# Sums of weight blocks issued behind the convolution's first closed token tile, or in the first feed-forward projection

## The chip, the cores and the metric

The kernel runs on one core of one Trainium2 chip. The metric is the device time of one execution in microseconds (us); the time of the kernel is the median over its runs. Engine names are those of the profile: PE multiplies matrices, PEld loads its weights, DVE, ACT and POOL compute, SP issues most of the loads from memory. POOL also issues transfers, in the same queue as its few computing instructions.

## The reference

Two layers over a residual stream of 512 tokens x 1024 features, all in float32. Layer 0 mixes with a gated short convolution, layer 1 with sliding-window attention; behind each mixer stands a gated feed-forward block.

```python
mix = short_conv_mixer(rmsnorm(h, a_pre_norm[l]), a_w_in[l], a_conv_w[l], a_w_out[l])
h = h + rmsnorm(mix, a_post_norm[l])
...
ff = swiglu(rmsnorm(h, ffn_pre_norm[l]), ffn_w_gate_up[l], ffn_w_down[l])
h = h + rmsnorm(ff, ffn_post_norm[l])
```

The change lies between the last product of layer 0's convolution (`y @ a_w_out`) and the first product of layer 0's feed-forward block (`rmsnorm(h) @ ffn_w_gate_up`).

## The kernel before

**Arithmetic.** Each float32 operand is split into a high and a low part (`whi`, `wlo`, `xhi`, `xlo`), and three products are added (`mm3`, L208 to L210). Most large products are made as seven block products instead of eight, which needs sums and differences of weight blocks. These sums are made in device memory by transfers alone: `Sums` holds, for one group of weights, two or four sum tiles (`hsum`), and a list of steps. The first step copies weight blocks into the sum tiles, the second adds other blocks to them (a transfer that accumulates), and two more steps add sums to sums where four are kept. A step must find the one before it landed.

**What sets when the sums are made.** `sum_on(at)` is called at named places. It issues what is left in `issues`, begins the sum group that the table `BEGIN` names for that place, and appends the next step of every open group to `issues`; these are issued by a later `issue` or `sum_on`. All of them go out on POOL's queue, on line L570, and are kept in program order. At `"o0"`, ahead of the convolution's closing, the group `g04` begins (gate weights, two sum tiles): its two copies are issued. At `"o1"` come the two accumulating transfers of `g04`, and the four copies of `d01` (a group of the down projection, four sum tiles): six transfers. At `"0f0"` comes the second step of `d01`, two accumulating transfers, which go out at the next place.

**The closing.** `close` multiplies the rest of the convolution's output with its weights, token tile by token tile (four tiles of 128 tokens, two halves of 512 features each; PE tile `pmix`). Each half is added to `mix` (`take`, L278, DVE) and squared on ACT (L283). `tile_done(t)` then runs, in this order:

```python
if t > 0: res.mean2(t - 1)   # uv L335 on DVE, then ur L339 on POOL
res.scale(t, 0)              # mix L309 on DVE
res.mean(t)                  # uv L312 on DVE, then ur L317 on POOL
if t > 0: res.norm(t - 1)    # xn L344 on ACT
res.scale(t, 1)
res.update(t)                # h L322 on DVE; kept L327 on SP's queue
if square: res.square(t)     # junk L330 on ACT
```

(comments by this text; `mean2` and `mean` take the power -1/2 of a mean square on POOL.) `mean` gives the factor with which tile t enters the residual stream, `mean2` the factor by which the updated tile is normalised into `xn`. So each of the four tiles sends two instructions of one column to POOL. In the last tile's second half PE does half of its products, then transposes `xn` of tiles 0 and 1 (`turn`, L355, 16 transposes into the banks `xt`), then the other half. ACT and DVE split the transposed tiles into high and low parts (`split`, L368 and L369).

**The first feed-forward projection.** `last_tile` finishes tiles 2 and 3 on the other engines while `project_first` runs plain products (PE tile `pgu`) over the first 256 tokens (`hf == 0`), block of features by block of features (`k`), and then over the last 256 (`hf == 1`); its callback `then(hf, k)` puts transposes and splits between. After that `in_line` runs a line of jobs, each with weight tiles (`raw`, fetched on SP's queue, L466) that are split on ACT (L499) and DVE (L500) three jobs ahead.

**Order.** On PE, DVE, ACT and POOL the instructions around the change stand in the order in which the code writes them. SP's queue is set by a scheduler.

Of the kernel before, what the change touches and what calls it, by code (L numbers as in the profile page):

```python
# [83 lines left out]
def yoco_kernel(  # L84
# [39 lines left out]
    def name(s):  # L124
        uid[0] += 1
        return f"{s}_{uid[0]}"
# [13 lines left out]
    def bank(s, pool=None):  # L140

        if pool is None:
            pool = (ps_mm, ps_sc, ps_mm, ps_pt)[turn[0] % 4]
            turn[0] += 1
        return pool.tile([P, S], F32, tag="bank", name=name(s))
# [413 lines left out]
    issues = []  # L559

    def issue(n, behind=None):

        for dst, src, op in issues[:n]:
            if len(dst.shape) == 3:
                dst, src = (t.rearrange("k (a b) c -> (k a) (b c)", b=4) for t in (dst, src))
            else:
                dst, src = (t.rearrange("(a b) c -> a (b c)", b=2) for t in (dst, src))
            kw = {} if op is None else {"accum_op": op}
            made = tc.keep_in_program_order(
                nc.gpsimd.dma_start(dst, src, max_dma_last_dim=4 * 4 * S, **kw))  # L570
            if behind is not None:
                tc.add_manual_dep(
                    made.ins, behind.ins.name, mybir.DependencyInfo(
                        mybir.DependencyClass.Sync, mybir.DependencyReason.DATA),
                    reason="pace")
        del issues[:n]
# [13 lines left out]
    def sum_on(at, behind=None):  # L590

        issue(len(issues), behind)
        if at in BEGIN:
            summing.append(sums_of[BEGIN[at]])
        for x in summing:
            x.step()
        summing[:] = [x for x in summing if x.steps]
# [38 lines left out]
    def seven(acts, n, mix, first):  # L636
# [9 lines left out]
        def product(p, ks, hi, lo):  # L646
# [35 lines left out]
    ws = [[wsp.tile([P, D], F32R, tag=tag, name=name(tag)) for tag in ("whi", "wlo")]  # L682
          for _ in range(3)]
# [104 lines left out]
    ws = [split_weights(None, raw, True) for raw in later[:2]]  # L788
# [33 lines left out]
    ys, acts, mix_c = [], [], [None] * NB  # L822
    both = []
    res = Update(mix_c, B_CONV, [G_FPRE[0]])
# [231 lines left out]
    ws = [line[f"w{n}"].w for n in range(4)]  # L1056
# [13 lines left out]
        if square:  # L1070
            res.square(t)

    def close(ws, x, k0, res, ahead, then=None, each=2, sooner=False):


        n = len(x) - k0

        def part(ps, t, half, ks):
            unit(ps, t, ws[len(ws) // 2 * half :], x, ks, n, k0)

        begun = [bank("pmix", ps_mm) for _ in range(2)]
        for half in range(2):
            part(begun[half], 0, half, range(n - 1))
            for _ in range(each if half == 0 or each > 1 else 0):
                ahead.one()
        for t in range(NB):
            for half in range(2):
                if t == 0:
                    ps = begun[half]
                    part(ps, t, half, range(n - 1, n))  # L1090
                else:
                    ps = bank("pmix", ps_mm)
                    if (t, half) == (NB - 1, 1):
                        lead = 3 if sooner else 2
                        part(ps, t, half, range(lead))
                        for ts in ((0,), (1,)) if sooner else ((0, 1),):
                            for b in range(4):
                                res.turn(b, ts)
                        part(ps, t, half, range(lead, n))
                        if sooner:  # L1100
                            res.split(0, 0, 0)
                            res.take(t, 0, last)
                            res.split(0, 1, 0)
                            res.take(t, 1, ps)
                            res.split(0, 2, 0)
                            res.split(0, 3, 0)
                            res.square_mix(t, 0)
                            res.square_mix(t, 1)
                            res.square(NB - 2)
                            continue  # L1110
                        for f in range(4):
                            res.split(0, f, 0)
                        res.square_mix(t, 0)
                        res.square(NB - 2)
                        res.scale(t, 0)
                    else:
                        part(ps, t, half, range(n))
                        if sooner and t == NB - 1:
                            last = ps
                            continue  # L1120
                res.take(t, half, ps)
                if (t, half) != (NB - 1, 0):
                    res.square_mix(t, half)
            if t < NB - 1:
                tile_done(res, t, square=t < NB - 2)
            if t == 0 and then:
                then()

    def last_tile(res, pieces, ahead=None):

# [42 lines left out]
    issue(len(issues))  # L1173
    ahead = Ahead(first_weights(0))
    with tc.manual_schedule(engines=ALL):

        def sums_on():
            sum_on("o1")
            issue(len(issues))

        close(ws, ys, 0, res, ahead, sums_on)


    def ffn(l, before, ahead, gain, gpres, following):
# [5 lines left out]
        def gate_pair(pg, pu):  # L1190
# [12 lines left out]
            return pair_sums(gr, acts[0])  # L1203

        def gate_jobs(q, factors, out, to, then):


# [141 lines left out]
        with tc.manual_schedule(engines=ALL):  # L1349
            last_tile(before, [  # L1350
                [(0, 4)], [(0, 5), ("keep", 0, False), ("weights",)],
                [], [("keep", 1, True), (0, 6), (0, 7), ("keep", 3, True)],
                [("keep", 2, False), ("weights",)]], ahead)

            def then(hf, k):
                if hf == 0 and k in (5, 6):
                    for b in ((0, 1), (2, 3))[k - 5]:
                        before.turn(b, (2,))
                if hf == 0 and k == 6:
                    for b in range(4):  # L1360
                        before.turn(b, (3,))
                    for f in range(KT):
                        before.split(0, f, 1)
                    for b in range(4):
                        before.keep(b, 1)
                if hf == 1 and k == 1:
                    factors.update(before.factors())
                if hf == 1 and k == 3:
                    sum_on(f"{l}f0")

            factors = {}
            project_first(pss, ahead.ready[:4], xs, then)

            def late():
                parts = [gate_pair(*pss[i : i + 2]) for i in (0, 2)][1]
                sum_on(f"{l}f1")
                return parts

            jobs, behind_one = [], []
            for rd, (f0, f1) in enumerate(ROUNDS):  # L1380
                last = rd == len(ROUNDS) - 1
                for f in range(max(f0, PLAIN), f1, 2):
                    q = (f - PLAIN) // 2
                    jobs += gate_jobs(q, factors, pair_acts if last else pair_sums, acts[rd],
                                      lambda q=q: sum_on(f"{l}p{q}"))
                    if behind_one and not (last and f < f1 - 2):
                        jobs += behind_one.pop()
                if last:
                    break
                down = down_jobs(range(f0 // 2, f1 // 2), acts[rd], rd == 0,  # L1390
                                 sums_of[f"d{l}{rd}"],
                                 lambda rd=rd: sum_on(f"{l}s{rd}"))
                behind_one.append(down)
            n = f1 - f0

            def weights(half, j):
                return w_dn[l, half : 4 - half : 3 - 2 * half, f0 // 2 + j]


            closing = [Job([Raw(weights(half, j))], None) for half in range(2) for j in range(2)]  # L1400
            for at, job in zip(LAST, closing):
                job.slots = True
                jobs.insert(len(jobs) - at, job)
            in_line(jobs, late)
            if l == 1:
                nc.gpsimd.drain()
        res = Update(mix, gain, gpres)
# [5 lines left out]
        ws = [job.w for job in closing]  # L1413
        if gpres:
            ahead = Ahead(following)
# [32 lines left out]
    res, ahead = ffn(0, res, ahead, B_FFN[0], [G_KV, G_BPRE], [  # L1448
        w_k[0], w_k[1], w_v[:, 0:D], w_v[:, D:], w_q[0], w_q[1]])
# [327 lines left out]
    with tc.manual_schedule(engines=ALL):  # L1777
        sum_on("a0")
        for i in range(KT + 2):
            if i == KT:  # L1780
                res = Update(mix_o, B_ATT, [G_FPRE[1]])
                res.leaves = True
                ahead = Ahead(first_weights(1))
# [5 lines left out]
            for c in order.split():  # L1789
# [18 lines left out]
                t = i - late  # L1808
# [19 lines left out]
                else:  # L1828
                    t = 2 * (t - EARLY - 1) + n.pop(0)
# [110 lines left out]
```

## Time and profile before

| | us |
|---|---|
| median of 3 runs | 1013.61 (1011.48 to 1014.05) |
| profiled execution | 1012.63 |
| its span, first to last instruction | 1010.9 |
| PE busy in it | 1000.5 |
| DVE, ACT, POOL busy | 911.2, 609.0, 182.9 |
| granted PE clock, mean | 0.998 of full |
| closing of the convolution (`pmix`) on PE | from 153.2 to about 179 |

The profiled execution took 1.7 us more than its span and 1.0 us less than the median. Times of single instructions are counted from the span's start. A busy PE counts each product to its modelled end, so that overlapping products make it look full.

### The profile page before, as it was taken

The page shows a single profiled execution, that of the slowest core. Times are in us where ns is not written, and L with a number is a line of the kernel's source. Part 1 is how long each engine was busy: PE and PEld are TensorE (multiplying, and loading weights), DVE is VectorE, ACT ScalarE, POOL GpSimd, SP SyncE. Part 2 cuts the span into 40 slices and gives each one's busy share as a digit, 9 for nine tenths or more (in the row PEclk, how much of TensorE's full clock was granted, in tenths as well). Part 3 has the DMA queues.
Part 4 walks back from the last instruction along what each step waited for, and adds up shares of the span by engine and source line. Part 5 has one row for each costly group of instructions (what it writes and reads, how often), then busy time and mean ns, then how long its engine had stood idle before and what let it go on. Part 6 is the DMA issues. An engine that isn't in the chain of part 4 may idle for free.

```text
span 1010.9 us, 16458 instructions
## 1 busy us (share of the span) xinstructions
PE 1000.5 (99%) x6008; PEld 887.4 (88%) x6008; DVE 911.2 (90%) x1564; ACT 609.0 (60%) x1105; POOL 182.9 (18%) x250
## 2 busy tenths in 40 slices
PE   9999999999999999999999999999999999999997
PEld 8899887999889898898898888789998888989986
DVE  7798876899789999999888998988997999999996
ACT  8345544875656465566385788777666564645641
POOL 0211022102101011000022657321211010110001
PEclk9999999999999999999999999999999999999999
DMA  9886989649979789779603889966999576979742
GB/s 353 265 239 179 334 285 319 199 167 270 341 235 286 252 286 311 238 219 341 209 1 121 225 223 258 293 242 173 306 294 316 167 250 233 295 264 275 242 170 83
DMA packets 67728, 246.61 MB, mean 244 GB/s; under 512 B 8000, under 2 KB 8512, under 8 KB 55872
## 3 DMA queue, kind: packets, MB, share of 16 engines
q1 hardware_dynamic: 52480, 148.07, 39.3%
q0 software_dynamic: 14592, 96.48, 37.3%
q8 instruction: 47, 0.77, 0.3%
q10 hardware_dynamic: 576, 1.02, 0.3%
q14 instruction: 33, 0.27, 0.1%
HBM read 239.25 MB, written 102.76 MB: 338 GB/s over the span
## 4 chain that ended last, share of the span: by engine, by line
PE 93%; DMA 3%; DVE 2%; ACT 1%; POOL 1%; issue 0%; DVEq 0%; ACTq 0%
PE gx L1284 15%; PE gx L1287 8%; PE px L208 4%; PE px L209 4%; PE px L210 4%; DMA hsum<-in_w_gb_dram 3%; PE gz L1284 3%; PE pmix L210 2%; PE gy L209 2%; PE gy L208 2%; PE gy L210 2%; PE pmix L208 2%; PE pmix L209 2%; PE pz L209 2%; PE pz L208 2%; PE pz L210 2%
## 5 line engine op out<-in xcount | busy, mean ns | idle before, releaser
L500 DVE TENSOR_TENSOR wlo<-raw,whi 128x1024 fp32r<-128x1024 f32 (+1 forms) x231 | 279.3, 1214 | 27.6 <-ACT whi L499 27.4
L499 ACT ACTIVATE whi<-raw 128x1024 fp32r<-128x1024 f32 (+1 forms) x231 | 239.7, 1051 | 79.1 <-DVE raw L487 37.7
L1284 PE MATMUL gx<-xt,whi 128*128 128x512 f32 x480 | 120.6, 393 | 0.0
L1284 PEld LDWEIGHTS gx<-xt,whi 128*128 128x128 f32 x480 | 86.2, 189 | 15.7
L570 POOL DMA_DIRECT2D hsum<-in_w_gb_dram x96 | 63.7, 730 | 167.8 <-ACT whi L499 107.6
L570 POOL DMA_DIRECT2D hsum<-hsum x32 | 25.2, 789 | 364.7 <-ACT whi L499 250.6
L1262 ACT ACTIVATE st<-gx 128x256 f32<-128x256 f32 x120 | 43.4, 380 | 60.9 <-PE gx L1287 57.3
L1239 DVE TENSOR_TENSOR st<-gx,st 128x256 f32<-128x256 f32 x200 | 77.6, 419 | 2.2 <-ACT st L1262 0.4
L1287 PEld LDWEIGHTS gx<-xt,wlo 128*128 128x128 f32 x480 | 65.5, 190 | 4.7
L1287 PE MATMUL gx<-xt,wlo 128*128 128x256 f32 x480 | 66.9, 282 | 0.0
L1298 ACT ACTIVATE gr<-gr 128x1024 f32<-128x1024 f32 x20 | 21.2, 1062 | 55.9 <-DVE gr L1239 55.9
L208 PE MATMUL gy<-xlo,whi 128*128 128x256 f32 x176 | 49.8, 283 | 0.0
L209 PE MATMUL gy<-xhi,whi 128*128 128x256 f32 x176 | 49.8, 283 | 0.0
L210 PE MATMUL gy<-xhi,wlo 128*128 128x256 f32 x176 | 49.8, 283 | 0.0
L208 PE MATMUL px<-wlo,ahi 128*128 128x512 f32 x120 | 46.7, 389 | 0.0
L209 PE MATMUL px<-whi,ahi 128*128 128x512 f32 x120 | 46.7, 389 | 0.0
L210 PE MATMUL px<-whi,alo 128*128 128x512 f32 x120 | 46.7, 389 | 0.0
L570 POOL DMA_DIRECT2D hsum<-in_w_dn_dram x48 | 31.8, 747 | 58.7 <-ACT whi L499 47.4
L1284 PE MATMUL gx<-xhl,whi 128*128 128x512 f32 x160 | 39.9, 391 | 0.0
L671 DVE TENSOR_TENSOR mix<-mix,px 128x512 f32<-128x512 f32 x54 | 34.8, 681 | 2.1 <-PE px L210 2.1
L317 POOL TENSOR_TENSOR ur<-uv,mhalf 128x1 f32<-128x1 f32 x15 | 13.8, 921 | 115.8 <-DVE uv L312 115.8
L487 DVE TENSOR_TENSOR raw<-raw,raw 128x1024 f32<-128x1024 f32 x28 | 34.1, 1219 | 0.1
(359 smaller groups left out, 3052.2 us busy)
## 6 DMA issues: line engine op xcount, KB each, us to landing
hsum<-in_w_gb_dram POOLq DMA_DIRECT2D x96, 512.0 KB, 7.9
raw<-hsum SPq DMA_DIRECT2D x88, 512.0 KB, 7.9
raw<-in_w_gb_dram SPq DMA_DIRECT2D x60, 512.0 KB, 7.0
hsum<-in_w_dn_dram POOLq DMA_DIRECT2D x36, 512.0 KB, 8.2
raw<-in_w_dn_dram SPq DMA_DIRECT2D x32, 512.0 KB, 6.5
hsum<-hsum POOLq DMA_DIRECT2D x28, 512.0 KB, 5.5
hsum<-in_w_dn_dram POOLq DMA_DIRECT2D x12, 768.0 KB, 13.8
raw<-in_w_in_dram SPq DMA_DIRECT2D x13, 512.0 KB, 7.2
```

The source lines that it names most:

```text
L208: nc.tensor.matmul(out, whi, xlo, start=start, stop=False, **kw)
L209: nc.tensor.matmul(out, whi, xhi, start=False, stop=False, **kw)
L210: nc.tensor.matmul(out, wlo, xhi, start=False, stop=stop, **kw)
L487: nc.vector.tensor_tensor(out=raw, in0=raw, in1=self.raws[1].tile, op=ALU.add)
L499: self.begun = nc.scalar.activation(hi[:, :n], raw, AF.Copy)
L500: nc.vector.tensor_tensor(out=lo[:, :n], in0=raw, in1=hi[:, :n].bitcast(F32), op=ALU.subtract)
L570: nc.gpsimd.dma_start(dst, src, max_dma_last_dim=4 * 4 * S, **kw))
L671: nc.vector.tensor_tensor(out=m, in0=m, in1=banks[bs][r], op=ALU.subtract if half else ALU.add)
L1239: nc.vector.tensor_tensor(out=out, in0=a, in1=b, op=ALU.add)
L1262: nc.scalar.activation(ste, a, AF.Copy)
L1284: nc.tensor.matmul(banks[c][e], whi[:, kk], factors[p][k][2], start=opened and k == 0, stop=False, **kw)
L1287: nc.tensor.matmul(banks[c][e][:, :256], wlo[:, kk], factors[p][k][0], start=False, stop=k == 3 and p in (4, 5), **kw)
```

## The change

The call at `"o1"` is no longer made behind token tile 0 of the convolution's closing; it is made in the first feed-forward projection of layer 0, at the second half's fourth feature block, right ahead of the call at `"0f0"`. The parameter that carried it into `close` is gone.

```diff
-    def close(ws, x, k0, res, ahead, then=None, each=2, sooner=False):
+    def close(ws, x, k0, res, ahead, each=2, sooner=False):
...
             if t < NB - 1:
                 tile_done(res, t, square=t < NB - 2)
-            if t == 0 and then:
-                then()
...
     with tc.manual_schedule(engines=ALL):
-
-        def sums_on():
-            sum_on("o1")
-            issue(len(issues))
-
-        close(ws, ys, 0, res, ahead, sums_on)
+        close(ws, ys, 0, res, ahead)
...
                 if hf == 1 and k == 3:
+                    if l == 0:
+                        sum_on("o1")
                     sum_on(f"{l}f0")
```

On POOL, at the end of token tile 0 of the convolution's closing, there stood before (`ur` are the one-column powers, L317 of `mean` and L339 of `mean2`; `hsum_142` and `hsum_143` are the sum tiles of `g04`, `hsum_164` to `hsum_167` those of `d01`; the names in brackets are what an instruction waits for, `DMASW` being earlier transfers of POOL's queue):

```order
L317 TENSOR_TENSOR ur_520<-uv_519,mhalf 128x1 [waits DVE_49]
L570 DMA hsum_142<-in_w_gb_dram 64x2048 [waits DMASW4_49]
L570 DMA hsum_143<-in_w_gb_dram 64x2048 [waits DMASW5_49]
L570 DMA hsum_164<-in_w_dn_dram 64x2048
L570 DMA hsum_165<-in_w_dn_dram 64x2048 [waits DMASW1_49]
L570 DMA hsum_166<-in_w_dn_dram 64x2048 [waits DMASW2_49]
L570 DMA hsum_167<-in_w_dn_dram 64x2048 [waits DMASW3_49]
L339 TENSOR_TENSOR ur_520<-uv_519,mhalf 128x1 [waits DVE_49]
```

Now, at the same place, with the two copies of `"o0"` ahead of it:

```order
L570 DMA hsum_142<-in_w_gb_dram 64x2048
L570 DMA hsum_143<-in_w_gb_dram 64x2048 [waits DMASW5_49]
L317 TENSOR_TENSOR ur_520<-uv_519,mhalf 128x1 [waits DVE_49]
L339 TENSOR_TENSOR ur_520<-uv_519,mhalf 128x1 [waits DVE_49]
L317 TENSOR_TENSOR ur_520<-uv_519,mhalf 128x1 [waits DVE_49]
```

The powers of tiles 0 to 3 now follow one another with no transfer between.

On POOL, behind the last power of the closing (`mean2` of tile 3), there stood before:

```order
L317 TENSOR_TENSOR ur_520<-uv_519,mhalf 128x1 [waits DVE_49]
L339 TENSOR_TENSOR ur_520<-uv_519,mhalf 128x1 [waits DVE_49]
L570 DMA hsum_164<-in_w_dn_dram 64x2048 [waits DMASW0_49]
L570 DMA hsum_165<-in_w_dn_dram 64x2048 [waits DMASW1_49]
L570 DMA hsum_166<-hsum_164 64x2048 [waits DMASW4_49,DMASW6_49,DMASW2_49,Activation_49]
```

Now:

```order
L317 TENSOR_TENSOR ur_520<-uv_519,mhalf 128x1 [waits DVE_49]
L339 TENSOR_TENSOR ur_520<-uv_519,mhalf 128x1 [waits DVE_49]
L570 DMA hsum_142<-in_w_gb_dram 64x2048 [waits DMASW4_49]
L570 DMA hsum_143<-in_w_gb_dram 64x2048 [waits DMASW5_49]
L570 DMA hsum_164<-in_w_dn_dram 64x2048
L570 DMA hsum_165<-in_w_dn_dram 64x2048 [waits DMASW1_49]
L570 DMA hsum_166<-in_w_dn_dram 64x2048 [waits DMASW2_49]
L570 DMA hsum_167<-in_w_dn_dram 64x2048 [waits DMASW3_49]
L570 DMA hsum_164<-in_w_dn_dram 64x2048 [waits DMASW0_49]
L570 DMA hsum_165<-in_w_dn_dram 64x2048 [waits DMASW1_49]
L570 DMA hsum_166<-hsum_164 64x2048 [waits DMASW4_49,DMASW6_49,DMASW2_49,Activation_49]
```

The six transfers moved past seven powers, in unchanged order among themselves, and carry no wait for the projection into whose code they were put. On PE, DVE, ACT and SP the order of the instructions is the same as before.

## The prediction

> **What bounds the kernel now.** I read the page's busy times first, then the waits of PE, then the chain that ended last around the place of the change, then the timelines of the engines on that chain.
>
> ```profile
> PE 1000.5 (99%) x6008; PEld 887.4 (88%) x6008; DVE 911.2 (90%) x1564; ACT 609.0 (60%) x1105; POOL 182.9 (18%) x250
> ```
> ```profile
> PE xt L355 <- ACT xn L344: 2.0, 1, 2.0
> PE idle L747 <- DVE ones L152: 1.1, 1, 1.1
> PE pt L1603 <- DVE plo L1620: 0.4, 1, 0.4
> ```
>
> PE is the bound, and in the whole span it waits three times. The longest, 2.0 us, is for `xn` at the transposes, and among the three it is the one in the convolution's closing. The chain shows what made `xn` late:
>
> ```profile
> 149.50 17.01 DMA hsum<-in_w_gb_dram
> 166.79 2.81 POOL hsum L570 x5
> 169.60 0.59 POOL ur L339
> ...
> 174.79 1.05 ACT xn L344
> ```
>
> A copy of `"o0"` takes 17 us to land; the accumulating transfer of `"o1"` waits for it on POOL; the next two powers (`mean2` of tile 0, then `mean` of tile 1) stand behind that; the update of tile 1, its `xn` and PE's transposes stand behind the powers. POOL's own timeline has it in order (start, duration, and in brackets the idle time before and who ended it):
>
> ```profile
> 164.94 0.83 POOL L570 DMA_DIRECT2D hsum<-in_w_gb_dram  x1 [3.20 <-DMA hsum<-in_w_gb_dram]
> 166.79 0.79 POOL L570 DMA_DIRECT2D hsum<-in_w_gb_dram  x1 [1.02 <-DMA hsum<-in_w_gb_dram]
> 167.31 2.29 POOL L570 DMA_DIRECT2D hsum<-in_w_dn_dram  x4
> 169.33 0.86 POOL L339 TENSOR_TENSOR ur<-uv,mhalf 128x1 f32<-128x1 f32 x1
> 169.88 0.84 POOL L317 TENSOR_TENSOR ur<-uv,mhalf 128x1 f32<-128x1 f32 x1
> ...
> 186.75 0.54 POOL L339 TENSOR_TENSOR ur<-uv,mhalf 128x1 f32<-128x1 f32 x1 [3.83 <-DVE uv L335]
> 187.25 1.64 POOL L570 DMA_DIRECT2D hsum<-in_w_dn_dram  x2
> ```
>
> **What is removed, step by step.** The operands of the two late powers had been ready for long:
>
> ```profile
> 164.93 0.14 DVE L335 TENSOR_SCALAR uv<-us 128x1 f32<-128x1 f32 x1
> 165.87 0.27 DVE L312 TENSOR_SCALAR uv<-us,epsv 128x1 f32<-128x1 f32 x1
> 170.75 1.29 DVE L322 SCALAR_TENSOR_TENSOR h<-mix,ur,h 128x1024 f32<-128x1024 f32 x1 [4.01 <-POOL ur L317]
> 171.95 1.28 DVE L278 TENSOR_TENSOR mix<-pmix,mix 128x512 f32<-128x512 f32 x2
> ```
>
> Step 1: without the six transfers, the power of tile 1's `mean` starts when its operand is there, at 165.87 + 0.27 = 166.1, and takes the 0.84 of the row at 169.88: done by 167.0. The update of tile 1 starts there and not at 170.75, 3.7 us sooner; this is nearly DVE's idle 4.01.
>
> Step 2: DVE then ends that update at 168.3, and takes the two halves of tile 2 (1.28 together). The second half is bounded by PE:
>
> ```profile
> 169.34 0.39 PE L210 MATMUL pmix<-whi,ylo 128*128 128x512 f32 x1
> 173.65 0.27 PE L355 MATMUL xt<-ident,xn 128*128 128x128 f32 x1
> 175.88 1.86 PE L355 MATMUL xt<-ident,xn 128*128 128x128 f32 x15 [1.97 <-ACT xn L344]
> 177.50 0.48 PE L208 MATMUL pmix<-wlo,yhi 128*128 128x512 f32 x1
> ```
>
> Its last product ends at 169.73, so DVE is through at about 170.4 where it was through at 171.95 + 1.28 = 173.23. Behind this point everything on DVE and ACT moves 2.8 us ahead. `xn` of tile 1 would end not at 175.84 (174.79 + 1.05) but at about 173.0. PE comes to the transposes at 173.65 as before, 0.6 us later. The wait is gone, with a small margin.
>
> Step 3, the price. Between the first transpose and the next product lie 177.50 - 173.65 = 3.85 us. The attention layer's closing has the same 16 transposes, and no transfer among its powers:
>
> ```profile
> 670.60 1.91 PE L355 MATMUL xt<-ident,xn 128*128 128x128 f32 x16
> 672.27 0.48 PE L208 MATMUL pmix<-wlo,ohi 128*128 128x512 f32 x1
> ```
>
> There they take 672.27 - 670.60 = 1.67 us. The gain on PE is 3.85 - 1.67 = 2.18 us; the bare wait (1.97) is the other estimate. I take 2.2, because the row is the same code without the stall.
>
> **What is late next.** PE is then 2.2 us ahead. The tightest hand-over that follows is the low part of feature block 6, which DVE makes right ahead of PE's use of it; first here, then in the attention layer:
>
> ```profile
> 187.37 0.87 DVE L369 SCALAR_TENSOR_TENSOR xlo<-xt,gt,xhi 128x256 fp32r<-128x256 f32 x2
> 187.94 0.36 PE L208 MATMUL pgu<-xlo,whi 128*128 128x256 f32 x1
> 681.55 0.87 DVE L369 SCALAR_TENSOR_TENSOR xlo<-xt,gt,xhi 128x256 fp32r<-128x256 f32 x2
> 682.72 0.36 PE L208 MATMUL pgu<-xlo,whi 128*128 128x256 f32 x1
> ```
>
> Half of the pair takes 0.44, so the margin here is 187.94 - 187.81 = 0.1 us. DVE moves 2.8 ahead and PE 2.2, which makes it about 0.7; the attention layer, where nothing delayed the powers, has 682.72 - 681.99 = 0.7. So no new wait there, and PE shows none later except the 0.4. All later work is released by earlier work of the same engines, so the 2.2 us should last to the end.
>
> **What is added at the new place.** The six transfers need about 4 us of POOL's time (0.83, 0.79 and 2.29 above). They stand behind the last power, 186.75 + 0.54 = 187.3, less 2.8: about 184.5 to 188.5. They wait for nothing (the copies of `"o0"` have landed by 166.8), and no power is queued behind them. Behind them stand `d01`'s two accumulating transfers, issued at 187.25 before. They must now wait until the copies have landed. The engines' capacity and the landing times:
>
> ```profile
> 160.00:170.00 10.00, 10.00 (x45) 8.26 (x45) 5.45 (x10) 3.01 (x8) 4.97 (x9) 1.00 1.03 383
> ...
> 180.00:190.00 10.00, 10.00 (x86) 10.00 (x85) 7.74 (x18) 8.86 (x19) 3.61 (x5) 1.00 0.62 219
> 190.00:200.00 10.00, 10.00 (x86) 10.00 (x85) 9.51 (x19) 8.38 (x21) 0.00 (x0) 1.00 0.68 151
> 200.00:205.00 5.00, 5.00 (x39) 4.78 (x38) 4.87 (x8) 2.92 (x5) 0.00 (x0) 1.00 0.00 0
> ```
> ```profile
> hsum<-in_w_dn_dram POOLq DMA_DIRECT2D x4, 512.0 KB, 12.7
> ```
> ```profile
> 297.52 2.37 SPq L466 DMA_DIRECT2D raw<-hsum  x2
> ```
>
> (The last two figures of a stretch are the share of the 16 transfer engines and GB/s.) Six times 512 KB are 3.1 MB, at the 383 GB/s of a full stretch 8.2 us. From 180 to 205 the engines have 3.8 + 3.2 + 5.0 = 12.0 us free, while 160 to 170 was full. So the transfers fit. Landing 12.7 us after 188.5, `d01`'s copies are there at 201; its accumulating transfers go out some 14 us later than before. The first of all the moved sums is fetched at 297.52 (the pair `hsum_142`, `hsum_143`). That is almost 100 us of cover, and I cost the delay at nothing.
>
> The cover that could fail is that of SP's two fetches in that stretch, for the second gate group:
>
> ```profile
> 186.35 0.33 SPq L466 DMA_DIRECT2D raw<-in_w_gb_dram  x1
> 191.08 0.33 SPq L466 DMA_DIRECT2D raw<-in_w_gb_dram  x1
> ```
> ```profile
> DMA to landing us min/median/max: 3.2/7.5/22.1
> ```
> ```profile
> 217.24 1.05 ACT L499 ACTIVATE whi<-raw 128x1024 fp32r<-128x1024 f32 x1
> 218.71 1.05 ACT L499 ACTIVATE whi<-raw 128x1024 fp32r<-128x1024 f32 x1
> ```
>
> Counted along the jobs, ACT splits these two at 217.24 and 218.71. Moved by 2.2, the fetches leave at 184.2 and 188.9 and are wanted at 215.0 and 216.5: they may take 30.8 and 27.6 us. The slowest weight fetch between 140 and 230 us took 22.1, in the fullest stretch of all. So 0 is my value; the far end is what a landing beyond 27.6 would cost, us for us.
>
> [...]
>
> **The sum.** -2.2 (wait gone) + 0 (POOL, sums) + 0 (fetches): the profiled execution goes from 1012.63 to 1010.4. The median of the runs stands 1.0 above that execution, so against 1013.61 I forecast 1011.4, 0.22% less. A difference of 0.3% (3.0 us) is about what a measurement of this kernel can tell from no change, so the gain lies inside it.
>
> **The rivals.**
> - The gain is only partial or vanishes. For it: the margins are 0.6 and 0.7 us. If DVE's chain moved less than I worked out, `xn` would again be last and PE would get only part of it; or a later hand-over takes it back. Against it: the attention layer runs this code with no wait. Price: between 0 and 2.2 less, 1011.9 to 1013.6. Chance 0.13.
> - Slower. The moved sums hold the two fetches of the second gate group until ACT wants them; PE then waits at that group's first products. It decides from a landing of 27.6 us on; to eat the gain and 3.0 more it must reach 27.6 + 2.2 + 3.0 = 32.8, when the time is 1016.6. For it: a fetch of 22.1 in a full stretch. Against it: the empty stretch from 200 to 205, and 6 us to go even from that worst row. Chance 0.07.
> - That the change doesn't move the stall (the wait has another cause than POOL) is counted in the first; the chain against it is unbroken from the transfer to PE.
>
> **How the numbers follow.** The forecast has 0.80. Its own range is 1010.1 to 1012.7, half the spread of the runs (1011.48 to 1014.05) to each side. It ends 0.8 us short of the 0.3% bound, so I give a third of its chance, 0.27, to a measured gain over 0.3%. Within 0.3% is the rest, 0.53, with the 0.13 and 0.01 of the slow rival: 0.67. Slower is 0.06. The range goes up to the case of no gain, 1013.6, and down a little beyond the forecast's own, to 1009.4, since medians of few runs scatter.
>
> **What would show it.** In the changed kernel, PE's waits should lack the 2.0 at the transposes, which stay at about 173.6 and take 1.7 us to the next product. DVE's idle 4.0 ahead of the update of tile 1 should shrink to some 0.4, with the two powers near 165.1 and 166.1. POOL should issue all six transfers between 184 and 189 with no wait, and the next two near 200. SP's two fetches should land later than before, with no engine waiting for them. I am wrong if PE waits anew for `xlo` or a weight split between 176 and 220, or if the transposes still wait for `xn`.

## The result and the profile after

The changed kernel takes 1009.74 us (median of 16 runs, 1009.3 to 1012.17), the kernel before 1012.63 (16 runs, 1010.68 to 1014.55). The ratio is 0.9974, 95% interval 0.9967 to 0.9982: 2.6 us less, with 1.8 and 3.3 as the ends. The profiled execution of the changed kernel took 1010.15 us, with a span of 1008.3.

PE's waits in the changed kernel; the one at the transposes is missing:

```profile
PE idle L747 <- DVE ones L152: 1.1, 1, 1.1
PE pt L1598 <- DVE plo L1615: 0.4, 1, 0.4
```

POOL's timeline in the changed kernel. The two powers start when DVE hands over their operands, the six transfers stand behind the last power, and it is now the two accumulating transfers of `d01` that wait, with no power of this stage behind them:

```profile
164.91 1.03 POOL L339 TENSOR_TENSOR ur<-uv,mhalf 128x1 f32<-128x1 f32 x1 [3.42 <-DVE uv L335]
165.97 0.92 POOL L317 TENSOR_TENSOR ur<-uv,mhalf 128x1 f32<-128x1 f32 x1
...
184.22 1.65 POOL L570 DMA_DIRECT2D hsum<-in_w_gb_dram  x2
185.32 2.55 POOL L570 DMA_DIRECT2D hsum<-in_w_dn_dram  x4
196.76 0.80 POOL L570 DMA_DIRECT2D hsum<-in_w_dn_dram  x1 [8.90 <-DMA hsum<-in_w_dn_dram]
198.08 0.79 POOL L570 DMA_DIRECT2D hsum<-in_w_dn_dram  x1 [0.51 <-DMA hsum<-in_w_dn_dram]
```

DVE's update of tile 1, ACT's `xn` of tile 1, and PE at the transposes, in the changed kernel:

```profile
166.92 1.28 DVE L322 SCALAR_TENSOR_TENSOR h<-mix,ur,h 128x1024 f32<-128x1024 f32 x1 [0.44 <-POOL ur L317]
```
```profile
171.37 1.15 ACT L344 ACTIVATE xn<-h,ur 128x1024 f32<-128x1024 f32 x1 [0.34 <-POOL ur L339]
```
```profile
173.40 1.91 PE L355 MATMUL xt<-ident,xn 128*128 128x128 f32 x16
175.06 0.48 PE L208 MATMUL pmix<-wlo,yhi 128*128 128x512 f32 x1
```

The update starts at 166.92 where it started at 170.75. `xn` is done at 172.5 (171.37 + 1.15), PE wants it at 173.4, and the transposes take 1.66 us up to the next product instead of 3.85.

### The profile page after: what moved, and what is told of

Read it like the earlier page. It is cut to its first block, busy times and chain, and to the rows that moved or that the text cites. A ratio compares the mean times of both kernels' runs of the same rounds, so it can differ in the third digit from the quotient of the medians.

```text
span 1008.3 us, 16458 instructions
## 1 busy us (share of the span) xinstructions
PE 999.9 (99%) x6008; PEld 887.4 (88%) x6008; DVE 911.2 (90%) x1564; ACT 609.4 (60%) x1105; POOL 184.1 (18%) x250
## 3 DMA queue, kind: packets, MB, share of 16 engines
q10 hardware_dynamic: 576, 1.02, 0.3%
## 4 chain that ended last, share of the span: by engine, by line
PE 97%; DVE 2%; ACT 1%; issue 0%; DVEq 0%
PE gx L1277 15%; PE gx L1280 8%; PE px L208 4%; PE px L209 4%; PE px L210 4%; PE pmix L210 3%; PE pmix L209 3%; PE pmix L208 3%; PE gz L1277 3%; PE pcub L208 2%; PE pcub L209 2%; PE pcub L210 2%; PE gy L209 2%; PE gy L208 2%; PE gy L210 2%; PE pz L208 2%
## 5 line engine op out<-in xcount | busy, mean ns | idle before, releaser
L317 POOL TENSOR_TENSOR ur<-uv,mhalf 128x1 f32<-128x1 f32 x15 | 13.9, 926 | 113.8 <-DVE uv L312 113.6
```

## The experiments

Two theories stood against each other. A: the powers stood in POOL's queue behind a transfer that waited for the landing of another (a transfer has landed when its data has arrived). B: the gain comes from taking six transfers out of a stretch in which the transfer engines were full (share 1.03 from 160 to 170 us).

**Only the two transfers that wait are moved.** Behind token tile 0 stay the four copies of `d01`:

```diff
-            sum_on("o1")
+            issue(len(issues))
+            summing.append(sums_of[BEGIN["o1"]])
+            summing[-1].step()
             issue(len(issues))
```

> Only the two accumulating transfers of the gate group, which wait for a landing, move to the later place; the four copies of the down group stay behind token tile 0. Theory A (the powers stand behind the landing wait on POOL): the four copies wait for nothing, go out between about 161.7 and 164.2, ahead of the operand of the next power at 165.1; PE's wait at the transposes is 0 and the ratio to before is that of the full change, 0.997 (-2.6 us). Rival B (the gain comes from taking load off the full stretch of transfers from 160 to 180): four of six transfers stay there, so a third of the gain, 0.999 (-0.9 us).

Measured: 1009.95 us against 1012.35 for the kernel before on the same chip, ratio 0.997 (0.9959 to 0.9982): the full gain with a third of the change. POOL's timeline in it shows the four copies between two powers, without harm:

```profile
161.22 2.03 POOL L570 DMA_DIRECT2D hsum<-in_w_dn_dram  x4
164.66 1.05 POOL L339 TENSOR_TENSOR ur<-uv,mhalf 128x1 f32<-128x1 f32 x1 [1.42 <-DVE uv L335]
```

They are issued by 163.3, and the power still waits 1.42 us for its operand. So four of the six transfers cost nothing in POOL's queue; the whole gain came with the two that wait.

**All six stay in the closing, one token tile later.**

```diff
-            if t == 0 and then:
+            if t == 1 and then:
                 then()
```

> All six transfers stay in the closing, but stand behind token tile 1 and not tile 0, so that they go out at about 167 to 171 where they went out at 165 to 170 before. Theory A: the two powers that were late go ahead of them; PE's wait is 0, the ratio 0.997 to 0.998 (-2.0 to -2.6 us); the next power (mean square of tile 1) may come up to 1 us late, which is hidden. Rival B: the transfers load the same stretch as before, so nothing is gained: ratio 1.000.

Measured: 1010.07 us, ratio 0.9973 (0.9962 to 0.9984). POOL in it:

```profile
165.22 0.92 POOL L317 TENSOR_TENSOR ur<-uv,mhalf 128x1 f32<-128x1 f32 x1
166.10 1.65 POOL L570 DMA_DIRECT2D hsum<-in_w_gb_dram  x2
167.21 2.55 POOL L570 DMA_DIRECT2D hsum<-in_w_dn_dram  x4
169.60 1.00 POOL L339 TENSOR_TENSOR ur<-uv,mhalf 128x1 f32<-128x1 f32 x1
```

The transfers leave in the stretch in which they left before (there 164.94 to 169.6), and the whole gain is there. B falls. The two accumulating transfers don't even wait here: they start at 166.10, right behind a power, with no idle time before them.

**A longer wait.** The copies of `"o0"` go out behind token tile 0, right ahead of the transfers that wait for them:

```diff
-    sum_on("o0")
-    issue(len(issues))
     ahead = Ahead(first_weights(0))
...
+            sum_on("o0")
             sum_on("o1")
```

> The two copies of the gate group no longer go out ahead of the closing but behind token tile 0, right ahead of the six transfers that wait for them; all else as before. Theory A: the copies leave at about 162 and land 8 to 17 us later, so the next power starts at 174 to 183 and not at 169.3; PE's wait at the transposes grows one for one, wait = start of that power - 167.4, so 7 to 15 us where it was 2.0; ratio 1.005 to 1.013. Rival B: the same transfers in the same stretch, two of them later and so less load ahead of it: no change or a gain, ratio 0.999 to 1.000.

Measured: 1017.38 us, ratio 1.0043 (1.003 to 1.0057). PE's wait (in two pieces, the longer 4.1 us) and POOL in it:

```profile
PE xt L355 <- ACT xn L344: 5.2, 2, 4.1
```
```profile
160.95 1.09 POOL L570 DMA_DIRECT2D hsum<-in_w_gb_dram  x2
167.60 0.81 POOL L570 DMA_DIRECT2D hsum<-in_w_gb_dram  x1 [5.56 <-DMA hsum<-in_w_gb_dram]
169.48 0.78 POOL L570 DMA_DIRECT2D hsum<-in_w_gb_dram  x1 [1.07 <-DMA hsum<-in_w_gb_dram]
...
172.01 0.86 POOL L339 TENSOR_TENSOR ur<-uv,mhalf 128x1 f32<-128x1 f32 x1
```

The direction is A's, the size was missed: the copies landed in an estimated 6.4 and 7.7 us and not in 8 to 17, so the power came at 172.0 instead of 174 to 183. (The estimate: the copies left at 160.95 and about 161.5, the transfers that wait for them started at 167.60 and 169.48, and in the kernel before such a start, at 166.79, came 0.28 us behind the landing at 149.50 + 17.01 = 166.51.) The rule given for the wait (start of the power less 167.4) gives 4.6 where 5.2 was measured. It ignored that the closing itself starts up to 1.2 us earlier or later in another execution; here it started at 152.48 where it had started at 153.24, and with this difference the rule gives 5.4.

**The wait without transfers.** The changed kernel, with idle powers on POOL behind token tile 0 (`spare` is a tile of one column that nobody reads):

```diff
+            if t == 0 and idle_powers:
+                for _ in range(idle_powers):
+                    nc.gpsimd.tensor_tensor(out=spare, in0=ones[:, :1], in1=mhalf[:, :1],
+                                            op=ALU.pow)
...
-        close(ws, ys, 0, res, ahead)
+        close(ws, ys, 0, res, ahead, idle_powers=14)
```

> The changed kernel (six transfers at the later place), with 14 powers of one column added on POOL behind token tile 0 whose result nobody reads; they hold POOL's queue as the wait did, and no transfer moves. Each takes 0.5 to 0.9 us, so POOL is free between 168.5 and 174. Theory A: PE's wait comes back, with wait = start of the next power - 167.4, so between 1 and 7 us; at a start of 169.3 it is the 2.0 of before and the ratio to before about 1.000. Rival B: the transfers are where the change put them, so the gain stays: ratio 0.997.

Measured: 1016.29 us, ratio 1.0032 to the kernel before (1.0019 to 1.0045). PE's wait, POOL, and the stretch from 176 to 180 us, around the end of the wait (its last three figures are granted PE clock as a share of full speed, share of the transfer engines, GB/s):

```profile
PE xt L356 <- ACT xn L345: 3.7, 1, 3.7
```
```profile
160.75 9.74 POOL L1129 TENSOR_TENSOR spare<-ones,mhalf 128x1 f32<-128x1 f32 x14
170.47 0.54 POOL L340 TENSOR_TENSOR ur<-uv,mhalf 128x1 f32<-128x1 f32 x1
```
```profile
176.00:180.00 4.00, 3.31 (x16) 3.31 (x17) 3.33 (x6) 2.06 (x4) 0.91 (x1) 0.50 0.23 96
```

The transfers stand where the change put them, and the wait is back: A is shown from the other side. But 6.5 us were lost against the changed kernel, to a wait of 3.75. The stretch shows where to look for the rest: the granted clock of PE is 0.50 there.

**The kernel before again, three times, and the changed one.** The runs of the kernel before scatter over 3.9 us; those of the changed kernel, but for one, over 1.1.

> The kernel before, unchanged, profiled again. Theory A with a wait that varies: the copies of the gate group land at another time in each execution, so the start of the second accumulating transfer and with it PE's wait at the transposes differ by 1 us or more between executions, and the time less that wait is the same within 0.5 us. Rival: PE's wait is 2.0 in each, and the scatter of the times before (1010.7 to 1014.6) comes from elsewhere.

> As the first repetition of the kernel before: a wait of PE that differs by 1 us or more from execution to execution, with time less wait the same within 0.5 us; the rival has 2.0 in each.

> As the first repetition of the kernel before: a wait of PE that differs by 1 us or more from execution to execution, with time less wait the same within 0.5 us; the rival has 2.0 in each.

> The changed kernel, unchanged, profiled again: no wait of PE at the transposes, and a span within 0.6 us of the first profile's 1008.3, which equals that of the kernel before less its wait.

Measured: 1013.97, 1013.84 and 1011.40 us for the kernel before, 1009.52 for the changed one (no wait at the transposes; its span of 1007.4 is 0.9 shorter than the first profile's, so the expected 0.6 was too narrow; all of the 0.9 lies ahead of the closing, which starts at 152.08 instead of 152.99). The expectation also has a sum wrong: 1010.9 less the wait of 1.97 is 1008.9, not 1008.3. PE's wait and the stretch behind it in the three, in that order:

```profile
PE xt L355 <- ACT xn L344: 2.5, 1, 2.5
```
```profile
176.00:180.00 4.00, 4.00 (x18) 3.77 (x18) 3.50 (x7) 2.58 (x7) 0.00 (x0) 0.59 1.02 426
```
```profile
PE xt L355 <- ACT xn L344: 2.4, 1, 2.4
```
```profile
176.00:180.00 4.00, 4.00 (x18) 3.62 (x17) 3.82 (x7) 3.11 (x7) 0.00 (x0) 0.57 1.03 423
```
```profile
PE xt L355 <- ACT xn L344: 1.0, 1, 1.0
```
```profile
176.00:180.00 4.00, 4.00 (x31) 3.75 (x29) 3.67 (x9) 3.13 (x8) 0.26 (x1) 1.00 1.01 420
```

The wait does vary, by 1.5 us. The time less the wait is not the same within the 0.5 us expected (1011.4, 1011.5, 1010.4), and the reason was not expected either: with the two longer waits the clock falls, with the shortest it doesn't.

**Two waits on either side of the fall.** The kernel with idle powers, with 11 and with 12 of them:

> The changed kernel with 11 instead of 14 idle powers behind token tile 0. In the runs so far PE's wait follows wait = (end of tile 1's mean power) - (first transpose) + 4.9 us, and an idle power took 0.70 us; so the wait is 3.75 - 3 x 0.70 = 1.7 us. Theory C (a wait longer than some 2.0 to 2.36 us also costs granted PE clock behind it): 1.7 is below that, the clock stays 1.00 and the closing is 1.9 us longer than in the changed kernel: 1011.6 us. Rival D (the extra cost grows in proportion with the wait, 6.5 us for 3.75 us): 2.9 us, 1012.7.

> The same with 12 idle powers: the wait is 2.4 us, 0.7 more than with 11. Theory C: 2.4 is above the bound, the granted clock falls to about half for some 3 us, and the closing is 4.2 us longer than in the changed kernel: 1014.0 us, 2.3 more than with 11 powers. Rival D (in proportion): 4.1 us here as well, but only 1.2 more than with 11 powers.

Measured: 1013.05 us with 11 (1011.44 to 1014.34, ratio 0.9998, 0.9986 to 1.001) and 1014.13 with 12 (1012.21 to 1015.35, ratio 1.0016, 1.0004 to 1.0029). PE's wait, the stretch behind it, and one product of the same kind behind the transposes, with 11 and then with 12 idle powers:

```profile
PE xt L356 <- ACT xn L345: 1.9, 1, 1.9
```
```profile
176.00:180.00 4.00, 4.00 (x32) 3.74 (x30) 4.00 (x8) 3.54 (x8) 0.00 (x0) 1.00 0.32 131
```
```profile
177.40 0.39 PE L210 MATMUL pmix<-whi,yhi 128*128 128x512 f32 x1
```
```profile
PE xt L356 <- ACT xn L345: 2.5, 1, 2.5
```
```profile
176.00:180.00 4.00, 4.00 (x20) 3.61 (x19) 3.88 (x7) 2.89 (x7) 0.00 (x0) 0.57 0.32 131
```
```profile
178.67 0.63 PE L210 MATMUL pmix<-whi,yhi 128*128 128x512 f32 x1
```

To put all profiles side by side I measure the closing on PE, from its first `pmix` product to the first `pgu` product. In the changed kernel:

```profile
152.99 0.39 PE L208 MATMUL pmix<-wlo,yhi 128*128 128x512 f32 x1
```
```profile
176.52 0.28 PE L208 MATMUL pgu<-xhl,whi 128*128 128x256 f32 x1
```

That is 23.53 us, and the same in its second profile.

| profile | PE's wait | closing | longer by | clock, 176 to 180 | time | time less "longer by" |
|---|---|---|---|---|---|---|
| changed | 0 | 23.53 | 0 | 1.00 | 1010.15 | 1010.2 |
| changed, again | 0 | 23.53 | 0 | 1.00 | 1009.52 | 1009.5 |
| two waiting transfers moved | 0 | 23.52 | 0 | 1.00 | 1010.13 | 1010.1 |
| one token tile later | 0 | 23.53 | 0 | 1.00 | 1009.51 | 1009.5 |
| before, third repetition | 1.03 | 24.78 | 1.25 | 1.00 | 1011.40 | 1010.2 |
| 11 idle powers | 1.94 | 25.70 | 2.17 | 1.00 | 1012.39 | 1010.2 |
| before, as predicted from | 1.97 | 25.72 | 2.19 | 1.00 | 1012.63 | 1010.4 |
| before, second repetition | 2.36 | 27.75 | 4.22 | 0.57 | 1013.84 | 1009.6 |
| 12 idle powers | 2.52 | 27.89 | 4.36 | 0.57 | 1014.15 | 1009.8 |
| before, first repetition | 2.54 | 27.95 | 4.42 | 0.59 | 1013.97 | 1009.6 |
| 14 idle powers | 3.75 | 30.03 | 6.50 | 0.50 | 1016.12 | 1009.6 |
| longer wait | 5.18 | 31.38 | 7.85 | 0.55 | 1017.90 | 1010.1 |

The last column stays within 0.9 us: the closing carries the difference between all these profiles. Up to a wait of 1.97 the closing is longer by the wait and 0.2; from 2.36 on it is longer by the wait and 1.8 to 2.8, and the clock has fallen. Between the profiles with 11 and 12 idle powers the wait grows by 0.58 us and the closing by 2.19, which speaks against a cost in proportion (3.4 us for a wait of 1.94, where 2.17 was measured).

The length of the fall can be estimated from stretches of 4 us, taking its clock as the 0.50 that the kernel with 14 idle powers shows from 176 to 180. With the waits of 2.36 and 2.52 us, 176 to 180 has a mean of 0.57, which is 3.4 us of fall; with the wait of 2.54 it has 0.59 and the stretch before it 0.98, 3.4 us together. With 14 idle powers the three stretches from 172 to 184 have 0.90, 0.50 and 0.75: 6.8 us, as one piece from 175.2 to 182.0. With the longer wait the two from 176 to 184 have 0.55 and 0.59: 6.9 us, from 176.4 to 183.3. Of these two falls the first 1.5 and 2.1 us lie inside the wait, which ended at 176.69 and 178.55. Behind the wait the products start 0.42 us apart with 12 idle powers (178.67 and 179.09) and 0.23 apart with 11 (177.40 and 177.63). If half of the time of the fall behind the wait is lost, that makes an estimated 1.7 us in the first three, 2.7 and 2.4 in the others. The table has 1.6 to 1.7, 2.5 and 2.5 beyond the wait and the 0.2. So the fall accounts for the rest.

The medians alone would not have decided: they differ by 1.1 us (1013.05 and 1014.13), where the fall in every run with 12 powers and in none with 11 asked for 2.3 and a cost in proportion for 1.2. But each run lists its mean granted clock. Among the profiles, every one with the fall has 0.997 or less and every one without it 0.998 or more. Sorted by this figure, the runs are in two groups with a gap between them:

| kernel | runs at 0.998 or 0.999: time | runs at 0.997 or less: time |
|---|---|---|
| changed, 16 runs | 16: 1009.30 to 1012.17 | none |
| 11 idle powers, 10 runs | 5: 1011.44 to 1012.71 | 5: 1013.38 to 1014.34 |
| 12 idle powers, 10 runs | 2: 1012.21 and 1012.53 | 8: 1014.07 to 1015.35 |
| before, beside these two, 18 runs (median 1013.66) | 8: 1010.37 to 1012.41 | 10: 1013.66 to 1014.69 |
| before, beside the first four experiments, 12 runs | 8: 1010.66 to 1013.05 | 4: 1013.67 to 1015.00 |

So, by the mean clock, half of the runs with 11 idle powers had the fall, and two of those with 12 escaped it; mainly for that reason the expected 1011.6 for 11 failed. In runs without a profile the fall itself is not seen, it is read from the mean clock alone. What stays open is how long the waits of these runs were, and so how sharp the bound is and what else decides near it.

## Why the prediction was right

- The stall and its cause. As forecast: the queue, the two powers (forecast 165.1 and 166.1, measured 164.91 and 165.97), DVE's idle time ahead of the update (0.4, measured 0.44), the transposes (1.67 us to the next product, measured 1.66). Two experiments moved less than the change and had all of its gain, and one brought the loss back without a transfer.
- The margins. `xn` came 0.9 us ahead of PE (forecast 0.6). The low part of feature block 6 came 0.74 ahead (forecast 0.7), in the changed kernel:

```profile
184.34 0.86 DVE L369 SCALAR_TENSOR_TENSOR xlo<-xt,gt,xhi 128x256 fp32r<-128x256 f32 x2
```
```profile
185.51 0.36 PE L208 MATMUL pgu<-xlo,whi 128*128 128x256 f32 x1
```

- The new place costs nothing that these profiles show. POOL issued the six transfers from 184.2 to 187.9 without a wait (forecast 184.5 to 188.5), and the two of `d01` at 196.8 and 198.1 (forecast near 200). The free stretch was used up: before, the share of the transfer engines was 1.01 from 170 to 180 and 0.00 from 200 to 205; in the changed kernel it is 0.28 and 0.91.

```profile
170.00:180.00 10.00, 10.00 (x68) 9.12 (x67) 7.71 (x16) 7.78 (x18) 3.37 (x4) 1.00 0.28 113
...
190.00:200.00 10.00, 10.00 (x86) 10.00 (x85) 9.27 (x17) 6.37 (x16) 1.59 (x2) 1.00 0.98 323
200.00:205.00 5.00, 5.00 (x37) 4.67 (x36) 4.27 (x7) 4.97 (x8) 0.00 (x0) 1.00 0.91 179
```

- The slow rival had no ground. SP's two fetches left at 183.3 and 188.1 and landed 3.7 and 8.8 us later, where ACT splits them at 214.8 and 216.3. The second was 1.3 us slower than before, the first not at all; both are nearer to the shortest landing before, 3.2, than to the 22.1 that spoke for this rival.
- The size. The forecast was 2.2 us; the ratio gives 2.6, the medians 2.9. The step that was too small is "the price" of the stall. 2.19 us is right for the execution that it was read from, as the table shows. But in the four profiled executions of the kernel before, the closing lost 1.25, 2.19, 4.22 and 4.42 us, and of its 30 later runs 14 have the lower mean clock that goes with the fall. The price was taken from one execution without the fall, and the sum had no term for the clock that a longer wait costs.
- The level. That the forecast time of 1011.4 lies above the measured 1009.74 has a second part: the sum started from a median of three runs, 1013.61, where sixteen gave 1012.63; this makes 1.0 of the 1.7 us. The measured time lies below the forecast's own range (1010.1 to 1012.7); it was inside the wider one only by the room down to 1009.4 that was given for scattering medians. The change was forecast by its mechanism, the level of the time was met with some luck.
- A slip. A gain that is smaller by 0 to 2.2 us gives 1011.4 to 1013.6, and not the 1011.9 to 1013.6 of the first rival; nothing else in the prediction rests on it.

## What to carry to other kernels

In this kernel a transfer that had to wait for another's landing held the instructions behind it on the issuing engine's queue (in the kernel before, waits of 3.20 and 1.02 us, and a power at 169.33 whose operand was there at 165.07), so it belonged behind the small latency-bound steps of the chain (those for whose result the next engine waits); one token tile later (1010.07 us) was as good as a whole stage later (1009.74). Where the runs of a kernel scatter, the profiled execution gives one length of a stall, not its price: profile it several times before sizing it, and compare the mean granted clock of the runs. Here a stall of the matrix engine cost more than its length once the clock fell with it: 4.22 us for a wait of 2.36.

## What the runs showed of the hardware

In the profiles of the table, the granted PE clock, as a mean from 176 to 180 us, was 0.50 to 0.59 with each wait of 2.36 us or more, and 1.00 with waits of 1.97 and less. By the estimate above it was low for 3.4 us with the waits of 2.36 to 2.54, and for 6.8 and 6.9 us with those of 3.75 and 5.18. A 128x512 product behind the transposes took 0.63 us with 12 idle powers and 0.39 with 11. The least that the fall cost was 1.6 us: between the waits of 1.97 and 2.36 the closing grew by 2.03 (4.22 less 2.19), of which 0.39 is the longer wait.

The landing of the same two 512 KB copies differed much: 15.7 and 17.0 us in the kernel before, when they left between 148 and 150 ahead of the closing, and an estimated 6.4 and 7.7 us with the longer wait, when they left at 161.
